# Loads of attention heads with the outermost dimension 64 or 128 in place of 2

## The chip, the cores and the metric

The kernel runs on one core of a Trainium2 chip. The metric is device time of one execution, in microseconds (us). Three runs of the kernel before took 3115.7, 3124.22 and 3126.91 us; their median is 3124.22. A core has five engines with queues of their own: PE (TensorE, matrix products; PEld is its weight load), DVE (VectorE), ACT (ScalarE), POOL (GpSimd) and SP (SyncE, which here only issues transfers). Transfers between the chip's memory and on-chip memory are issued from SP or from POOL and are carried out by 16 DMA engines, which both share.

## The reference

Two decoder layers over 1024 positions of width 1024, in float32. Each layer is a token mixer, a cross-attention into 256 memory rows, and a SwiGLU FFN, with an RMS norm before each and a residual add after. The mixers are:

```python
# layer 0: 8 heads with a sliding window of 128, and 8 MLA heads (dense causal)
s = (jnp.einsum('bqhd,bkhd->bhqk', q_nope[:, q0:q1], k_nope[:, :q1])
     + jnp.einsum('bqhd,bkd->bhqk', q_rope[:, q0:q1], k_rope[:, :q1])).astype(jnp.float32) * scale
p = jax.nn.softmax(jnp.where(causal, s, -jnp.inf), axis=-1).astype(v.dtype)
# layer 1: 16 heads, each a mixture of three dilated windows
DIL_PATTERNS = ((128, 1), (512, 4), (2048, 16))
o, lse = banded_attention(deinterleave(q), deinterleave(k), deinterleave(v), window // dil)
```

Heads are 64 wide; the rotary part of an MLA head is 32 wide (two halves of 16), and its keys are shared by all heads.

## The kernel before, in words

**Precision by splitting.** Each float32 operand x is held as a high part (rounded) and a low part (x minus the high part). A product takes the terms high by high, high by low and low by high. A score is a product over the 64 rows of a head, and PE has 128 rows. So the kernel puts the key's high rows on 64 partitions and its low rows on the other 64 (`kf`), and the query's high rows on all 128, each twice (`q[0]`). One matrix product then gives both terms with the high query; a second one with the query's low rows, again twice (`q[1]`), gives the rest. For an MLA head a third product adds the rotary part: `qr` holds 16 + 16 rotary rows, high and low, each half of them twice, against `KR`. A product is a sum over partitions, so the order of the rows is free as long as keys and queries have the same one.

**Through memory.** Projections write keys to `kd` ([pair of heads, 128 rows, high/low, position]), queries to `qd` ([pair, 128 rows, half, high/low and position]), rotary queries to `qrd`, values to `vd` and `vd1`. The attention then loads them head by head, all with `move` (L175), which issues the transfer on POOL's queue.

**Passes.** The sequence is worked in halves of 512 positions (`hf` 0 and 1): layer 0 first half, layer 0 second half, layer 1 first half, layer 1 second half. In each pass two streams are woven on PE by `g_weave`: "s", attention and the rest of the mixer, and "d", dense work (projections of the other half, or the FFN of the half before). In the rows of the profile `s<-...` and `d<-...` say which stream a product is of. The loads that change belong to:

- `g_mla` (layer 0, 8 heads, both halves): per head one key load, one query load, two rotary loads and one value load, into the tiles `ar` and `qr`;
- `g_att1` (layer 1, first half, 16 heads) and `g_dil` (layer 1, second half, 16 heads): per head one key and one query load, into slices of `tab`, besides value loads.

Scores are at L744 (`g_scores`) and, in `g_dil`, at L1466. Keys and queries have two buffers each, so the load of head n + 1 or n + 2 is issued once the scores of the head before are done.

**What sets the order.** The kernel is written as one sequence; a scheduler with a timing model of its own then orders each engine's queue, and after that every queue runs strictly in order. POOL's queue holds three sorts of work: the issue of its transfers, the low parts of weights (`wl<-wr,wh`, L181 in `lo`), and some scaling in the attention. Weights come through SP's queue (L210), ACT makes the high part (L212) and POOL the low part. Transfers from POOL share eight semaphores in turn (DMASW0 to 7), and each waits for the one eight before it.

Of the kernel before, what the change touches and what calls it, by code (L numbers as in the profile page):

```python
# [19 lines left out]
S = 1024  # L20
# [142 lines left out]
class Builder:  # L163
# [552 lines left out]
    def form_k(self, m, src, n):  # L716

        k = m.kf.next()[:, :n]
        self.move(k, src.rearrange("d j t -> j d t"))
        return k  # L720

    def form_q(self, m, src):

        q = m.q.next().rearrange("p (j t) -> p j t", j=2)
        self.move(q, src[None].to_broadcast([2, 64, 1024]))
        return q[:, 0], q[:, 1]

    def form_v(self, m, src, nb):
# [575 lines left out]
    def g_mla(self, hf):  # L1304

        nc, I, s = self.nc, self.I, self.S
        with ExitStack() as es:
            ext = self.pool(es, f"ml{hf}", 1)
            m = self.att_mem(hf, ext, True)
            W = 512 * (hf + 1)  # L1310
            KR = ext.tile([P, W], F32R, name="KR")
            self.move(KR, self.krd[:, 0:W])
            nc.sync.dma_start(m.bias, I["c_mla"][:, S - W:])

            def head(hd):
                def f():
                    kf = self.form_k(m, self.head(self.kd, 8 + hd, slice(0, W)), W)
                    q = self.form_q(m, self.queries(8 + hd, hf))

                    qr = m.qr.next()  # L1320
                    v = self.qrd[hf, hd // 4].rearrange("(x h) j f t -> h x (j f) t", x=2)[hd % 4]
                    for a in range(2):
                        self.move(qr[64 * a:64 * a + 64], v[a][None].to_broadcast([2, 32, 512]))
                    vf = self.form_v(m, self.vd[8 + hd][:, 0:W // P, :], W // P)
                    return [(q[0], kf), (q[1], kf), (qr, KR)], vf
                return f

            yield from self.g_heads(s, m, hf, [(head(hd), 512 + 64 * hd) for hd in range(8)], m.bias, SC96)
# [14 lines left out]
    def load1(self, m, hd, hf):  # L1343

        if hf:
            k, q = m.kq.next()
            self.move(k, self.head(self.kd, hd, slice(0, S)).rearrange("d j t -> j d t"))
            self.move(q, self.queries(hd, 1)[None].to_broadcast([2, 64, 1024]))
            return k, q.rearrange("p (j t) -> p j t", j=2)
        kf = self.form_k(m, self.head(self.kd, hd, slice(0, 512)), 512)  # L1350
        q = self.form_q(m, self.queries(hd, 0))
        return [(x, kf) for x in q], self.values1(m.vf.next()[:, :512].rearrange("p (b d) -> p b d", d=P), hd, 0)
# [410 lines left out]
```

## Time and profile before

| | |
|---|---|
| median of three runs | 3124.22 us |
| the profiled execution | 3122.54 us, span 3120.6 us |
| mean granted TensorE clock | 0.955 |
| PE busy | 2844.0 us (91%) |
| DVE busy | 1809.0 us (58%) |
| POOL busy | 1489.9 us (48%) |
| ACT busy | 1307.6 us (42%) |
| transfers issued by POOL | 169.92 MB, 18.8% of 16 engines' span |
| transfers issued by SP | 245.67 MB, 27.7% of 16 engines' span |

A row of a group gives line, engine, operation, the tiles written and read, the count, busy time and the mean of one. A row of waits gives who waited, for whom, us in total, times, and the longest. A row of DMA issues gives the tiles, the queue, the count, the size of one transfer and the median time from issue to landing. In a table by windows each row is a stretch of time: its length, then busy time and instructions of each engine, the granted clock of PE, the mean busy share of the 16 DMA engines, and GB/s.

### The profile page before, as it was taken

What the parts mean: (1) busy time and instruction counts of PE and PEld (TensorE: products, weight loads), DVE (VectorE), ACT (ScalarE), POOL (GpSimd) and SP (SyncE); (2) the same over time, 40 slices, a digit from 0 to 9 for tenths busy, and PEclk for the clock granted to TensorE, in tenths of its full rate; (3) what the DMA queues carried; (4) which work ended last, traced back from release to release, by engine and by line L of the source; (5) the groups of instructions that cost most, each with busy time, mean ns of one, the idle gap of its engine ahead of it and who ended that gap; (6) DMA issues with size and microseconds to landing.
All of it is one profiled execution on the core that took longest, in us unless ns stands there. A gap on an engine that the chain in (4) does not pass through costs nothing. (4 is left out here: it accounts for less than half of the span.)

```text
span 3120.6 us, 37882 instructions
## 1 busy us (share of the span) xinstructions
PE 2844.0 (91%) x13500; PEld 2365.7 (76%) x13500; DVE 1809.0 (58%) x3668; ACT 1307.6 (42%) x2539; POOL 1489.9 (48%) x1038
## 2 busy tenths in 40 slices
PE   6866898889999999998899999988889999999998
PEld 5655777768888788876777787866778887878887
DVE  6764766657676564455566646335668865562324
ACT  4644534444443333453444333345455533432222
POOL 3564635554354444644455444444465654444442
PEclk9978999999999999998999999989999999999999
DMA  6666744554453324544555333454555553333331
GB/s 176 173 186 154 224 133 139 144 133 116 119 153 121 109 88 128 165 160 117 131 120 171 115 108 102 144 163 148 129 141 154 137 165 105 109 119 101 95 97 65
DMA packets 467135, 418.00 MB, mean 134 GB/s; under 512 B 114884, under 2 KB 377284, under 8 KB 466948
## 3 DMA queue, kind: packets, MB, share of 16 engines
q1 hardware_dynamic: 333124, 245.67, 27.7%
q0 software_dynamic: 133824, 169.92, 18.8%
q8 instruction: 107, 1.75, 0.2%
q14 instruction: 80, 0.66, 0.1%
HBM read 347.09 MB, written 68.03 MB: 133 GB/s over the span
## 5 line engine op out<-in xcount | busy, mean ns | idle before, releaser
L181 POOL TENSOR_TENSOR wl<-wr,wh 128x1024 fp32r<-128x1024 f32 (+1 forms) x430 | 1036.3, 2417 | 987.6 <-ACT wh L212 924.6
L212 ACT ACTIVATE wh<-wr 128x1024 fp32r<-128x1024 f32 (+1 forms) x418 | 440.4, 1056 | 843.7 <-PE d L236 229.0
L236 PE MATMUL d<-hfh,wh 128*128 128x512 f32 x1408 | 564.1, 401 | 1.8 <-DVE ra L361 1.8
L236 PE MATMUL d<-hfl,wh 128*128 128x512 f32 x1408 | 558.9, 397 | 0.0
L236 PE MATMUL d<-wh,a 128*128 128x512 f32 x1440 | 532.9, 401 | 28.1 <-ACT a L693 13.4
L236 PE MATMUL d<-hfh,wl 128*128 128x512 f32 x1408 | 558.0, 397 | 0.0
L660 DVE TENSOR_TENSOR x<-d,x 128x512 f32<-128x512 f32 x344 | 233.9, 685 | 300.9 <-PE d L236 299.6
L236 PEld LDWEIGHTS d<-wh,a 128*128 128x128 f32 x1440 | 274.4, 191 | 90.2 <-ACT a L693 14.6
L236 PEld LDWEIGHTS d<-hfh,wl 128*128 128x128 f32 x1408 | 269.2, 191 | 54.7
L236 PEld LDWEIGHTS d<-hfh,wh 128*128 128x128 f32 x1408 | 269.2, 191 | 51.1 <-DVE x L660 2.0
L236 PEld LDWEIGHTS d<-hfl,wh 128*128 128x128 f32 x1408 | 269.5, 191 | 49.8 <-issue 0.2
L236 PE MATMUL d<-wl,a 128*128 128x512 f32 x720 | 283.9, 396 | 0.0
L660 DVE TENSOR_TENSOR x<-s,x 128x512 f32<-128x512 f32 x192 | 130.6, 688 | 116.9 <-PE s L236 115.3
L181 DVE TENSOR_TENSOR a<-t,a 128x512 fp32r<-128x512 f32 x104 | 160.5, 1544 | 53.2 <-ACT a L693 51.2
L236 PEld LDWEIGHTS d<-wl,a 128*128 128x128 f32 x720 | 137.7, 191 | 24.8
L757 ACT ACTIVATE af<-af,nm 128x512 f32<-128x512 f32 (+3 forms) x160 | 94.1, 589 | 139.3 <-DVE nm L753 138.8
L687 DVE SCALAR_TENSOR_TENSOR t<-t,d 128x512 f32<-128x512 f32 x88 | 60.2, 685 | 110.2 <-ACT t L686 109.8
L236 PE MATMUL s<-hmh,wl 128*128 128x512 f32 x256 | 103.8, 406 | 20.1 <-POOL wl L181 20.0
L181 DVE TENSOR_TENSOR pl<-s,ph 128x512 fp32r<-128x512 f32 (+1 forms) x158 | 97.4, 629 | 32.8 <-ACT ph L184 32.2
L184 ACT ACTIVATE ph<-s 128x512 fp32r<-128x512 f32 (+1 forms) x158 | 84.2, 550 | 75.5 <-PE s L780 71.7
L753 DVE CUSTOM_DVE_ANT_0 af<-s,bias 128x512 f32<-128x512 f32 (+3 forms) x128 | 67.3, 534 | 79.8 <-PE s L744 50.2
L236 PE MATMUL s<-hmh,wh 128*128 128x512 f32 x256 | 102.5, 400 | 4.9 <-ACT wh L212 4.9
(360 smaller groups left out, 5727.4 us busy)
## 6 DMA issues: line engine op xcount, KB each, us to landing
wr<-in_l_w_gate SPq DMA_DIRECT2D x88, 512.0 KB
wr<-in_l_w_up SPq DMA_DIRECT2D x88, 512.0 KB
wr<-in_l_w_down SPq DMA_DIRECT2D x88, 512.0 KB
wr<-in_l_w_qkv SPq DMA_DIRECT2D x48, 512.0 KB
wr<-in_l_w_out SPq DMA_DIRECT2D x32, 512.0 KB
tab<-qd POOLq DMA_DIRECT2D x32, 512.0 KB, 17.0
ar<-qd POOLq DMA_DIRECT2D x24, 512.0 KB, 17.9
wr<-in_l_w_in SPq DMA_DIRECT2D x22, 512.0 KB
```

Of the source, the lines that this page charges most:

```text
L181: e.tensor_sub(out, x, h.bitcast(F32))
L184: self.nc.scalar.activation(h, ps, AF.Copy)
L212: self.nc.scalar.activation(h, raw, AF.Copy)
L236: self.nc.tensor.matmul(ps, a, b, start=(3 * i + j == 0), stop=(3 * i + j == n - 1))
L660: self.nc.vector.tensor_add(xs, ps, xs)
L687: nc.vector.scalar_tensor_tensor(t, t, 1.0, pg, op0=ALU.add, op1=ALU.mult)
L753: nc.vector.tensor_tensor_reduce(p[:, c:c + n], t, bias[:, b0 + c:b0 + c + n], -scale, lim, ALU.add, ALU.min, accum_out=nm)
L757: nc.scalar.activation(p[:, c:c + n], p[:, c:c + n], AF.Exp, bias=nm, scale=-1.0, accum_out=l[:, i:i + 1])
```

## The change

All loads of keys, queries and rotary queries of a head in `g_mla`, `g_att1` and `g_dil` are issued with another order of rows.

- **Keys.** Before, the source ran over high/low (2), then the head's rows (64). Now it runs over 128 rows, high and low of one row next to each other. Partition 2d holds row d's high part and partition 2d + 1 its low part.
- **Queries.** Before, the source was repeated by an outermost dimension of 2 with a step of zero. Now the repeat stands inside: 64 rows, each read twice.
- **Rotary parts.** Before, two loads per head, each of 32 rows repeated twice by an outermost 2 into 64 partitions. Now four loads of 32 rows into 32 partitions each. The place of the rows is as before.

Bytes, descriptors per row and products are the same; per MLA head there are two more transfers (32 in all).

```diff
     def form_k(self, m, src, n):
         k = m.kf.next()[:, :n]
-        self.move(k, src.rearrange("d j t -> j d t"))
+        self.move(k, src.rearrange("d j t -> (d j) t"))
         return k
 
+    @staticmethod
+    def twice(src):
+
+        return src[:, None].to_broadcast([64, 2, 1024])
+
     def form_q(self, m, src):
         q = m.q.next().rearrange("p (j t) -> p j t", j=2)
-        self.move(q, src[None].to_broadcast([2, 64, 1024]))
+        self.move(q, self.twice(src))
         return q[:, 0], q[:, 1]
...
                     v = self.qrd[hf, hd // 4].rearrange("(x h) j f t -> h x (j f) t", x=2)[hd % 4]
-                    for a in range(2):
-                        self.move(qr[64 * a:64 * a + 64], v[a][None].to_broadcast([2, 32, 512]))
+                    for a in range(4):
+                        self.move(qr[32 * a:32 * a + 32], v[a // 2])
...
         if hf:
             k, q = m.kq.next()
-            self.move(k, self.head(self.kd, hd, slice(0, S)).rearrange("d j t -> j d t"))
-            self.move(q, self.queries(hd, 1)[None].to_broadcast([2, 64, 1024]))
+            self.move(k, self.head(self.kd, hd, slice(0, S)).rearrange("d j t -> (d j) t"))
+            self.move(q, self.twice(self.queries(hd, 1)))
```

The scheduler orders the queues anew. Line numbers from L724 on are five higher in the changed kernel.

On POOL in layer 0, first half, from the second head's loads (`qr_1726`) on, before:

```order
L177 DMA qr_1726<-qrd 64x1x512 x2
L177 DMA ar<-vd 128x512
L181 TENSOR_TENSOR wl<-wr,wh 128x1024
L177 DMA mkv_109<-a_1989 128x256 x2
L181 TENSOR_TENSOR wl<-wr,wh 128x1024
L177 DMA ar<-kd 128x1x512
L177 DMA ar<-qd 128x1x1024
L177 DMA qr_1725<-qrd 64x1x512 x2
L177 DMA ar<-vd 128x512
L815 DMA OTd<-af 64x512
L181 TENSOR_TENSOR wl<-wr,wh 128x1024
```

and now:

```order
L177 DMA qr_1726<-qrd 32x512 x4
L177 DMA ar<-vd 128x512
L181 TENSOR_TENSOR wl<-wr,wh 128x1024 x2
L177 DMA mkv_109<-a_1995 128x256 x2
L177 DMA ar<-kd 128x512
L177 DMA ar<-qd 128x1x1024
L177 DMA qr_1725<-qrd 32x512 x4
L177 DMA ar<-vd 128x512
L177 DMA ar<-kd 128x512
L177 DMA ar<-qd 128x1x1024
L177 DMA qr_1726<-qrd 32x512
L820 DMA OTd<-af 64x512
```

The loads of the third and fourth head now stand together, where a weight's low part stood between them before.

On PE at the same place, where the dense stream turns to the second half's activations (`hBh`, `hBl`), the rows between a tile's first two terms and its third. Before there are 30 rows, of which the first and last are:

```order
L236 MATMUL d<-hBh,wh 128x512
L236 MATMUL d<-hBl,wh 128x512
L744 MATMUL s<-ar 128x384 x2
L744 MATMUL s<-KR,qr_1726 128x384
L628 MATMUL d<-wl,mem 128x512
...
L791 MATMUL s<-ph_1727,ar 128x256
L792 MATMUL s<-ph_1727,ar 128x256
L236 MATMUL d<-hBh,wl 128x512
```

and now there are 50, all of them of stream "s":

```order
L236 MATMUL d<-hBh,wh 128x512
L236 MATMUL d<-hBl,wh 128x512
L796 MATMUL s<-ph_1728,ar 128x256
L797 MATMUL s<-ph_1728,ar 128x128
L785 MATMUL s<-ident,af 128x128 x4
...
L799 MATMUL s<-pl_1730,ar 128x256
L785 MATMUL s<-ident,af 128x128 x4
L236 MATMUL d<-hBh,wl 128x512
```

So for the length of about two heads no dense product stands between the attention's.

In layer 1 POOL's queue keeps its order. Around the load of the second head's queries in the first half it reads, before:

```order
L177 DMA tab<-qd 128x1x1024
L177 DMA qd<-hl 128x1024
L181 TENSOR_TENSOR wl<-wr,wh 128x1024 x3
L177 DMA tab<-kd 128x1x512
L177 DMA tab<-qd 128x1x1024
```

and now:

```order
L177 DMA tab<-qd 128x1x1024
L177 DMA qd<-hl 128x1024
L181 TENSOR_TENSOR wl<-wr,wh 128x1024 x3
L177 DMA tab<-kd 128x512
L177 DMA tab<-qd 128x1x1024
```

Nothing moved there; a store of the last queries (`qd<-hl`) still stands right behind a load.

## The prediction

> **What bounds the kernel now.** I read the page first, then PE's waits.
>
> ```profile
> span 3120.6 us, 37882 instructions
> PE 2844.0 (91%) x13500; PEld 2365.7 (76%) x13500; DVE 1809.0 (58%) x3668; ACT 1307.6 (42%) x2539; POOL 1489.9 (48%) x1038
> ```
>
> PE sets the time, since no other engine is near it; a change that removes no product can win only where PE stands still or runs slowly. It stands still for 3120.6 - 2844.0 = 277 us. Waits of PE over the whole span (who, for whom: us in total, times, longest):
>
> ```profile
> PE s L744 <- DMA ar<-qd: 21.2, 4, 13.4
> PE s L1466 <- DVE de L1468: 15.1, 3, 8.5
> PE d L236 <- ACT wh L212: 14.6, 1, 14.6
> PE d L236 <- ACT a L693: 13.4, 3, 7.7
> PE s L1466 <- DMA tab<-qd: 13.3, 4, 6.7
> PE s L744 <- DMA tab<-qd: 13.3, 3, 6.7
> PE s L744 <- DMA ar<-qrd: 9.7, 1, 9.7
> PE s L744 <- DVE nm L753: 6.9, 1, 6.9
> ```
>
> The rows with DMA are scores that wait for a head's loads: 21.2 + 13.3 + 13.3 + 9.7 = 57.5 us. The others I follow below. Next, how long these loads take (DMA issues; the last column is the median from issue to landing):
>
> ```profile
> tab<-qd POOLq DMA_DIRECT2D x32, 512.0 KB, 17.0
> ar<-qd POOLq DMA_DIRECT2D x24, 512.0 KB, 17.9
> wr<-OTd POOLq DMA_DIRECT2D x16, 512.0 KB, 4.5
> qd<-hl POOLq DMA_DIRECT2D x16, 512.0 KB, 2.9
> tab<-kd POOLq DMA_DIRECT2D x16, 512.0 KB, 16.3
> qr<-qrd POOLq DMA_DIRECT2D x16, 128.0 KB, 16.7
> ```
>
> At equal size from the same queue, those that change take 16 to 18 us, others 3 to 5. DMA queues between 250 and 257 us, when almost only such a load was under way, say why:
>
> ```profile
> q0 software_dynamic: 165, 0.35, 13.7%
> q1 hardware_dynamic: 171, 0.09, 4.2%
> ...
> 1305.00:1306.00 1.00, 1.00 (x6) 0.81 (x5) 0.00 (x0) 0.99 (x2) 1.00 (x1) 1.00 0.98 385
> ```
>
> (The last row is a window, with a store of keys under way; its last two numbers are the DMA engines' share and GB/s. A store has 128 rows outermost, and fills all 16 engines.) POOL's queue q0 used 13.7% of 16 engines, about 2.2 of them, as many as the source's outermost dimension has steps. SP's queue q1, with a weight to bring at the same time, moved 0.09 MB in 7 us: its shares on those two engines take turns with the load's rows, and a weight is there only when its last share is.
>
> So three more of PE's waits belong to the loads. The chain of waits (start, us, what) has the store in front of the dilated pass, and a weight there beside one outside it:
>
> ```profile
> 2158.26 11.80 DMA qd<-hl
> ...
> 2292.67 13.64 DMA wr<-in_l_w_up
> ...
> 2562.17 3.62 DMA wr<-in_l_w_out
> ```
>
> POOL's timeline around the first, and SP's in the pass before:
>
> ```profile
> 2154.14 0.83 POOL L177 DMA_DIRECT2D tab<-qd  x1 [2.31 <-DVE t L508]
> ...
> 2158.26 0.56 POOL L177 DMA_DIRECT2D qd<-hl  x1 [0.86 <-DVE hl L181]
> 2170.71 3.09 POOL L177 DMA_DIRECT2D v<-vd  x5 [11.89 <-DMA qd<-hl]
> ...
> 1414.84 0.82 POOL L177 DMA_DIRECT2D tab<-qd  x1
> 1417.54 0.56 POOL L177 DMA_DIRECT2D qd<-hl  x1 [1.88 <-DVE hl L181]
> ...
> 1431.90 0.34 SPq L1420 DMA_DIRECT2D bias<-in_c_dil  x1
> ```
>
> A store issued behind a query load took 11.80 us in place of 2.9, and what reuses its room waited: at 2171 us the 8.5 of "DVE de L1468", at 1435 us, through the mask's load, the 6.9 of "DVE nm L753". The weight that took 13.64 us ends in the 7.7 of "ACT a L693"; the 14.6 of "ACT wh L212" is the weight that crawled at 250 us. Together 8.5 + 6.9 + 7.7 + 14.6 = 37.7 us, and with the direct waits 95.2.
>
> Last, the clock. Four stretches, each right behind a stall but the first, which is one (length; busy; granted clock sixth):
>
> ```profile
> 212.21:225.65 13.44, 0.00 (x1) 0.03 (x1) 0.00 (x0) 1.06 (x1) 0.66 (x1) 0.60 0.63 132
> 225.65:242.30 16.65, 11.80 (x42) 9.74 (x43) 11.06 (x20) 4.71 (x12) 10.50 (x11) 0.50 0.79 159
> 259.25:262.90 3.65, 3.65 (x10) 3.12 (x11) 2.98 (x6) 1.49 (x6) 2.36 (x1) 0.51 0.05 14
> 282.70:286.70 4.00, 4.00 (x17) 3.81 (x18) 0.78 (x2) 1.19 (x2) 3.59 (x3) 0.50 0.44 105
> 670.00:1110.00 440.00, 421.15 (x2123) 354.32 (x2122) 269.75 (x528) 181.71 (x356) 185.97 (x120) 0.98 0.44 122
> ```
>
> After stalls of 13.4, 14.6 and 6.7 us PE ran at half clock for 16.65, 3.65 and 4.0 us, which costs half of that, 12.1 us for 34.7 of stall: 0.35 us for each us.
>
> **The change, part by part.** *Keys and queries.* 48 heads load both. With 64 or 128 steps outermost I expect all 16 engines and the landing of the spread rows: 512 KB in 2.9 to 4.5 us, so a pair in about 6 where it took 18. The source of a query with a repeat of 2 inside is a form that no row of before has; its bounds are 4.5 us and the 17.9 of now, and I take 4.5, as its outermost dimension is that of the stores. The Trainium skill, page "DMA: Bandwidth & Descriptors", section "Why a DMA increments its semaphore by 16 and not by 1", says a transfer takes the largest number of engines up to 16 that divides the outermost size on both sides. By it the old loads get 2, as the trace shows, and the new 16.
>
> The issues cost POOL less, if anything (least, median, most in ns):
>
> ```profile
> L177 POOL DMA_DIRECT2D tab<-vd x64: 548/552/785, 1267.8 to 1679.3; - x64
> L177 POOL DMA_DIRECT2D tab<-qd x32: 782/810/978, 1321.5 to 2447.2; - x32
> L177 POOL DMA_DIRECT2D qr<-qrd x16: 653/664/886, 205.8 to 326.8; - x16
> L177 POOL DMA_DIRECT2D qd<-hl x16: 559/572/698, 1309.9 to 2158.3; - x16
> ```
>
> At the store's 572 ns 48 queries give back 48 x 0.24 = 11 us of POOL, at 810 nothing.
>
> *Rotary loads.* 32 more issues at 552 to 664 ns are 18 to 21 us of POOL in layer 0. They lie in time in which POOL is idle (it is busy for 186 of the 440 us from 670 on) and PE has the dense stream; without that cover they would cost these 21 us. Each transfer waits for the one eight before it, and a head now has seven and not five. Landing in 6 us at most, against eight issues of 0.6, that does not bind; at today's 17 it would, and does now:
>
> ```profile
> POOL qr L177 <- DMA ar<-qd: 21.0, 3, 9.3
> ```
>
> Against the split speaks the same page, section "Rules for kernel authors": small transfers are mostly overhead, and halves of the partitions are better moved in one. By its fixed 2.0 us, paid one after the other, two more loads cost 4 us a head, an estimate, seen by PE only at the first head of each half: 8 us less gain.
>
> *Order.* Layer 1 keeps POOL's order, so there the stalls can go with nothing else moved. In layer 0 the first half is woven anew, with 50 rows of attention in one piece, where PE has nothing to fill the softmax's latency.
>
> *The sum*, in gaps plus 0.35 of them for the clock:
> - layer 0, first half: 21.2 + 14.6 = 35.8, with clock 48. I take half, 24, for the new order.
> - layer 0, second half: 9.7, with clock 13. I take 10; the first load is issued just before its use and still needs some 6 us.
> - layer 1, first half: 13.3 + 6.9 = 20.2, with clock 27.
> - layer 1, second half: 13.3 + 8.5 + 7.7 = 29.5, with clock 40.
>
> Of the last two I take three quarters, 20 + 30, between the ends: all of it, and half of the direct waits alone, without clock (29 us over all passes). The nearer row is the one from 670 to 1110 us: the same sort of loads, issued a head early, and beyond the first load's 9.7 PE stands still for 9 of 440 us. What is late next is the softmax's chain on DVE, which is why it is not all. Sum: 24 + 10 + 20 + 30 = 84 us; 3122.5 - 84 = 3038.5 for the profiled execution, which ran 1.7 us below the median of the runs. I predict 3040.
>
> **The rivals.**
> *Another engine takes over.* In the dilated pass DVE is the next:
>
> ```profile
> 2146.00:2483.00 337.00, 296.60 (x1516) 255.12 (x1515) 240.23 (x635) 175.93 (x463) 179.83 (x157) 0.93 0.55 142
> ```
>
> It is busy for 240 of 337 us, and PE already waits for it there (15.1 above). If a DVE wait steps into each gap's place, half of the direct waits return and no clock: 3122.5 - 29 = 3094. Against it: 71% leaves a quarter free. 0.16.
>
> *The queries stay on few engines*, because the repeat inside counts. Then keys and rotary parts are quick, but the score still waits for the queries; issued 0.8 us behind the keys, they now end the waits. About a quarter of the ceiling of 128 returns, from lighter traffic on the two engines: 3122.5 - 32 = 3091; with queues no better, 3110. 0.05.
>
> *Slower.* Layer 0's new order decides: weights' low parts stand behind two heads of loads (14 issues x 0.65 = 9 us), and the dense stream, cut off for two heads, comes late. If each of the eight heads of the first half got a gap like the 14.6 with its clock, 20 us, that is 160 in place of the 48 there now: 112 lost, against 60 gained elsewhere, about 3175. It decides from the point where the first half grows by more than layer 1 gives back, some 50 us. Against it: the dense products only move within the pass, and the loads that delayed POOL get short. 0.04.
>
> *No change*: the scores wait as long for something not seen. 0.05.
>
> **How the numbers follow.** The forecast holds 0.70: its own range is 2994 (the whole ceiling of 95.2 x 1.35 = 128) to 3080. With the case of 3094 the range is 2992 to 3095. A measurement here tells 0.5%, 16 us: faster means below 3108.6. Forecast, most of the takeover and the queries' case lie there: 0.91. Within: 0.05. Slower: 0.04.
>
> **What would show it.** The issue rows of `tab<-qd`, `ar<-qd` and `tab<-kd` at 3 to 7 us, and q0's share up in short bursts; PE's waits on DMA down from 57.5 to below 15; the store before the dilated pass near 3 us; weights there at 4; the clock's mean from 0.955 to 0.97 or more. Landing rows that stay near 17 for queries show the second rival; quick landings with PE waiting for DVE rows instead show the first. The prediction is wrong if loads land fast and the time stays above 3095.

## The result and the profile after

The changed kernel takes **2977.94 us** (median of 4 runs, 2975.36 to 2979.06) against 3121.96 us for the kernel before in the same runs: a ratio of **0.9539**, 95% interval 0.9519 to 0.9558. The forecast was 3040, range 2992 to 3095. The sign was right; 144 us were gained, not 84, and also more than the 128 that the prediction held to be all there was.

From the page of the changed kernel, the span and the engines:

```profile
span 2976.7 us, 37929 instructions
PE 2819.6 (95%) x13500; PEld 2350.7 (79%) x13500; DVE 1790.7 (60%) x3668; ACT 1309.3 (44%) x2539; POOL 1478.8 (50%) x1070
```

PE's idle time fell from 276.6 to 157.1 us. The other 24.4 us are PE's busy time, 2844.0 to 2819.6 for the same 13500 products: the granted clock (mean 0.955 before, 0.973 now). PE's waits over the whole span (who, for whom: us in total, times, longest), the largest, the dilated pass's, and all on heads' loads:

```profile
PE s L399 <- DVE xn L416: 39.1, 14, 9.0
...
PE s L1471 <- DVE de L1473: 7.2, 2, 4.3
...
PE s L749 <- DMA ar<-qrd: 1.7, 1, 1.7
...
PE s L1254 <- DMA ar<-qd: 0.7, 1, 0.7
...
PE s L749 <- DMA qr<-qrd: 0.7, 1, 0.7
```

(Lines after L724 moved by five: L744 is L749 now, L1466 is L1471.) The 57.5 us of direct waits on loads that the prediction counted (59.4 with two more rows of 1.6 and 0.3) became 3.1. The DMA issues, last column the median from issue to landing:

```profile
tab<-qd POOLq DMA_DIRECT2D x32, 512.0 KB, 5.6
ar<-qd POOLq DMA_DIRECT2D x24, 512.0 KB, 7.4
...
tab<-kd POOLq DMA_DIRECT2D x16, 512.0 KB, 5.0
...
qr<-qrd POOLq DMA_DIRECT2D x32, 64.0 KB, 6.3
```

Keys and queries of 512 KB land in 5 to 7 us where they took 16 to 19, the queries with their repeat inside too. (8 of the 24 loads in the row `ar<-qd` are of the sliding-window heads and did not change.)

**Where the time went.** Stretches between the same instructions in both kernels (length; busy time and instructions of PE, PEld, DVE, ACT, POOL; granted clock; DMA share; GB/s): layer 0 first half, layer 0 second half, layer 1 first half, layer 1 second half (attention stages). Before:

```profile
198.10:674.30 476.20, 395.32 (x1899) 328.60 (x1898) 294.81 (x628) 210.05 (x438) 241.72 (x201) 0.89 0.56 157
674.30:1307.10 632.80, 610.59 (x2978) 510.49 (x2977) 366.00 (x682) 251.32 (x459) 282.84 (x174) 0.98 0.45 126
1307.10:1682.30 375.20, 329.50 (x1540) 270.58 (x1539) 215.45 (x431) 165.22 (x315) 183.19 (x162) 0.94 0.49 132
2044.60:2516.90 472.30, 415.79 (x2036) 351.31 (x2035) 311.14 (x739) 244.09 (x572) 248.39 (x210) 0.93 0.53 143
```

and after:

```profile
201.50:659.50 458.00, 403.63 (x1909) 330.29 (x1908) 286.89 (x631) 213.12 (x440) 246.01 (x218) 0.91 0.54 164
659.50:1284.10 624.60, 610.22 (x2969) 509.60 (x2968) 360.34 (x680) 250.46 (x456) 283.65 (x190) 0.99 0.41 127
1284.10:1591.70 307.60, 306.30 (x1534) 258.42 (x1533) 210.13 (x431) 165.06 (x315) 175.26 (x163) 1.00 0.52 162
1954.80:2373.70 418.90, 402.99 (x2036) 344.34 (x2035) 312.42 (x739) 243.55 (x572) 240.21 (x210) 0.99 0.52 161
```

Against the prediction's terms:

| stage | predicted | measured | of it idle time | of it busy time |
|---|---|---|---|---|
| layer 0, first half | 24 | 18.2 | 26.5 | -8.3 |
| layer 0, second half | 10 | 8.2 | 7.8 | 0.4 |
| layer 1, first half | 20 | 67.6 | 44.4 | 23.2 |
| layer 1, second half | 30 | 53.4 | 40.6 | 12.8 |
| elsewhere | 0 | -3.5 | | |
| sum | 84 | 143.9 | | |

Layer 1 gave 121 of the 144. Its first half shows why the count was short. PE's waits there, before, the seven largest:

```profile
PE s L744 <- DMA tab<-qd: 13.3, 3, 6.7
PE s L744 <- DVE nm L753: 6.9, 1, 6.9
PE s L236 <- POOL wl L181: 6.6, 4, 3.8
PE d L236 <- ACT a L693: 5.6, 2, 3.2
PE s L791 <- ACT ph L184: 3.8, 1, 3.8
PE s L793 <- DVE pl L181: 3.5, 2, 1.8
PE s L236 <- ACT wh L212: 2.4, 3, 1.7
```

and all that is left of them:

```profile
PE d L236 <- DVE a L181: 0.7, 1, 0.7
PE d L236 <- DVE t L687: 0.6, 1, 0.6
```

The prediction had counted the first two rows, 20.2 us. The other five name POOL, ACT and DVE, come to 21.9 us, and went as well, though nothing was changed on these engines.

What these engines themselves waited for in layer 1, up to the end of the dilated pass (1307.1 to 2516.9 us before, 1284.1 to 2373.7 after), went too. ACT waited 93.8 us for weights to land, the largest row "ACT wh L212 <- DMA wr<-in_l_w_up: 64.9, 12, 9.4", and now 15.2. POOL stood 34.5 us before loads until a store of queries had landed ("POOL tab L177 <- DMA qd<-hl: 22.6, 2, 14.0" and 11.9 of `v`), and now 9.1.

### The profile page after: what moved, and what is told of

It is laid out like the page before. It is cut to its first block, busy times and chain, and to the rows that moved or that the text cites. A ratio compares the mean times of both kernels' runs of the same rounds, so it can differ in the third digit from the quotient of the medians.

```text
span 2976.7 us, 37929 instructions
## 1 busy us (share of the span) xinstructions
PE 2819.6 (95%) x13500; PEld 2350.7 (79%) x13500; DVE 1790.7 (60%) x3668; ACT 1309.3 (44%) x2539; POOL 1478.8 (50%) x1070
## 5 line engine op out<-in xcount | busy, mean ns | idle before, releaser
L212 ACT ACTIVATE wh<-wr 128x1024 fp32r<-128x1024 f32 (+1 forms) x418 | 440.1, 1056 | 738.9 <-PE d L236 248.2
L181 DVE TENSOR_TENSOR pl<-s,ph 128x512 fp32r<-128x512 f32 (+1 forms) x158 | 97.7, 631 | 46.7 <-ACT ph L184 46.0
L399 PE MATMUL s<-ident,xn 128*128 128x128 f32 x384 | 62.8, 310 | 41.9 <-DVE xn L416 39.1
L236 PE MATMUL s<-hml,wh 128*128 128x512 f32 x256 | 100.3, 392 | 0.0
```

Of the source, the lines that this page charges most:

```text
L181: e.tensor_sub(out, x, h.bitcast(F32))
L212: self.nc.scalar.activation(h, raw, AF.Copy)
L236: self.nc.tensor.matmul(ps, a, b, start=(3 * i + j == 0), stop=(3 * i + j == n - 1))
L399: self.nc.tensor.transpose(v[:, k, :], xn[:, (k0 + k) * P:(k0 + k + 1) * P], self.ident)
```

## The experiments

Two questions were left. Did those waits on other engines go because of the loads, although no engine waited for a load there? And why did layer 0 give so little?

### One layer alone

Layer 1 as changed, layer 0's loads as before (`layer1_only`). Every product on PE stands in the order of the kernel before.

```diff
 # in g_mla
-                    kf = self.form_k(m, self.head(self.kd, 8 + hd, slice(0, W)), W)
-                    q = self.form_q(m, self.queries(8 + hd, hf))
+                    kf = m.kf.next()[:, :W]
+                    self.move(kf, self.head(self.kd, 8 + hd, slice(0, W)).rearrange("d j t -> j d t"))
+                    q = m.q.next().rearrange("p (j t) -> p j t", j=2)
+                    self.move(q, self.queries(8 + hd, hf)[None].to_broadcast([2, 64, 1024]))
+                    q = q[:, 0], q[:, 1]
...
-                    for a in range(4):
-                        self.move(qr[32 * a:32 * a + 32], v[a // 2])
+                    for a in range(2):
+                        self.move(qr[64 * a:64 * a + 64], v[a][None].to_broadcast([2, 32, 512]))
```

> Layer 1's loads as in the change, layer 0's as before. Theory: layer 1's two passes give 67 and 53 us by the marks of the two traces, whatever layer 0 does: 3122 - 120 = 3002 us, within 6. Rival (part of layer 1's gain is carried over from layer 0, for instance by the place at which the streams meet): 3020 or more.

Measured: 3004.46 us, ratio 0.9618 (0.9596 to 0.9639), within the theory's 6 us. With nothing moved in PE's order, layer 1's loads alone are worth 119 us. So layer 1's gain owes nothing to a new order.

### Two-engine copies that nobody waits for

To the changed kernel, one copy of the head's queries into a spare tensor per head and half of layer 1, 512 KB each, 32 in all. In `extra2` the outermost dimension is 2, as the old loads had it; in the control `extra64` it is 64; in `extra2_act` the two-engine copies are issued from ScalarE, so that they stand in a queue of their own.

```diff
+            self.move(self.spare[hf, hd], self.queries(hd, hf)[None].to_broadcast([2, 64, 1024]))   # extra2
+            self.move(self.spare[hf, hd], self.twice(self.queries(hd, hf)))                         # extra64
+            self.nc.scalar.dma_start(...)     # extra2_act: as extra2, from ScalarE's queue
```

> The changed kernel plus, for each head and half of layer 1, a copy of the head's queries (twice, 512 KB) into a tensor that nobody reads, with an outermost dimension of 2: the old loads' confinement to two DMA engines with no engine waiting for it. 32 copies, 16.8 MB. Theory (a two-engine transfer takes turns with the weights on the same engines and stretches them, and so costs the 24 us of waits in layer 1's first half that the profile put on ScalarE, VectorE and GpSimd and that went with the loads): 3000 to 3040, weights landing in over 8 us instead of 4, and the loss is in layer 1's two attention stages. Rival (only a wait on the load itself costs anything): within 8 us of the control with the same copies over 16 engines.

> The control to the run with the extra two-engine copies: the same 32 copies of the same bytes at the same places, with an outermost dimension of 64. The order of TensorE's work is the same in both. Theory: the bytes alone cost little, 2975 to 2995; what the other run takes above this one is the price of the two engines alone, with no direct wait in it.

> The run with the 32 extra two-engine copies in layer 1 (3079 us; its control over 16 engines 2984), with the copies issued by ScalarE into its own DMA queue instead of GpSimd's: no store and no load of a head stands behind a copy in a queue any more, and what is left is that two DMA engines are shared with the weights and everything else. The scheduler's order of layer 1 differs a little, and ScalarE has 32 issues more. Theory 1 (the sharing of the engines does most of the harm): 3040 to 3085, and weights still wait. Theory 2 (standing in the same queue does it: stores that take 16 us instead of 6 and the loads behind them): 2980 to 3005, with the stores of keys and queries back at 3 to 6 us. In between the loss divides accordingly.

Measured: `extra64` 2983.60 us (0.9561, 0.9547 to 0.9576), `extra2` 3078.73 (0.9867, 0.9852 to 0.9881), `extra2_act` 3163.19 (1.013, 1.0092 to 1.0168). The bytes cost some 6 us (the intervals overlap, and PE's order in layer 1 is not quite the changed kernel's); the same bytes on two engines cost 95 us more, with every engine's queue in the same order; from a queue of their own some 180 us more than the control. The 95 us lie far beyond the 3000 to 3040 of `extra2`'s theory: the mechanism was expected, its size was not. Two thirds of the change's gain are given back by copies whose data nobody uses; a single wait on a copy, 6.1 us of a store on POOL, is in the trace.

PE's waits from 1280 to 2500 us in `extra2`, the rows that grew most and the one on a load:

```profile
PE s L236 <- ACT wh L212: 23.9, 9, 4.6
PE s L1473 <- DVE de L1475: 21.0, 3, 13.2
PE s L236 <- POOL wl L181: 16.0, 10, 2.3
PE s L796 <- ACT ph L184: 9.3, 1, 9.3
...
PE s L1473 <- DMA tab<-qd: 4.4, 1, 4.4
```

and in the control:

```profile
PE s L1473 <- DVE de L1475: 13.0, 4, 4.3
...
PE s L236 <- POOL wl L181: 6.8, 7, 2.3
...
PE s L236 <- ACT wh L212: 0.2, 1, 0.2
```

Only 4.4 of the 95 us stand in a row that names a load. The rest stands in rows of ACT, DVE and POOL, the sorts of rows that the prediction had left out, and in the clock. Two paths show. One is the queue. The DMA issues of `extra2`:

```profile
spare<-qd POOLq DMA_DIRECT2D x32, 512.0 KB, 14.8
...
kd<-hl POOLq DMA_DIRECT2D x16, 512.0 KB, 15.8
qd<-hl POOLq DMA_DIRECT2D x16, 512.0 KB, 11.1
```

The stores of keys and queries took 6.4 and 3.9 us in the control. They stand behind a copy. POOL's queue, being in order, then stands still as well, where a copy is issued only when a store of queries has landed. POOL's waits from 1280 to 2500 us in `extra2` hold the row

```profile
POOL spare L177 <- DMA qd<-hl: 89.9, 12, 10.7
```

and the control's is 19.0 us. So much of it belongs to the experiment: in the kernel before, waits of this sort came to the 34.5 us above. The other path is the two engines. In `extra2_act` no store stands behind a copy and the two kinds of store land in 7.1 and 6.9 us, but ACT's and SP's waits from 1270 to 2600 us are

```profile
ACT wh L212 <- DMA wr<-in_l_w_qkv: 119.0, 14, 18.4
...
SPq L210 <- DMA wr<-in_l_w_qkv: 114.9, 12, 16.5
```

and PE waits 99.1 us for the high parts of weights:

```profile
PE s L236 <- ACT wh L212: 99.1, 14, 16.5
```

The chain of waits there (start, us, what) shows single weights that take 27 and 33 us:

```profile
1298.29 32.60 DMA wr<-in_l_w_qkv
...
1334.54 26.69 DMA wr<-in_l_w_qkv
```

From 1316 to 1320 us, with nothing but copies and the rest of a weight under way, the queues (packets, MB, share of 16 engines) were

```profile
q10 hardware_dynamic: 46, 0.19, 11.4%
q1 hardware_dynamic: 45, 0.02, 1.8%
```

q10 is ScalarE's queue: 11.4% of 16 engines is 1.8 engines, and the weights' queue q1 moved 0.02 MB in 4 us, about one packet of its own, of 512 B, for each of the copies', of 4 KB. So theory 1 of that run held, beyond the loss that it gave (3040 to 3085): sharing two engines does harm without a queue in common. The 180 us are not all its doing, though. PE's order in layer 1 differs from the control's. And ACT, which makes the weights' high parts, was itself held by the issue of its copies: 10 of the 32 took 1.1 to 12.0 us in place of 0.58, together 43 us more, for a reason that no row gives. Why the copies do more harm from ScalarE's queue than from GpSimd's, where they also have to wait behind stores and loads, no run tells. Nor is it shown how PE's loss in layer 1 of the kernel before divided between the two paths.

The idle time that `extra2` adds to the control in layer 1's two stages, and the busy time that comes with it (`extra2` first, then the control):

```profile
1277.50:1635.60 358.10, 320.30 (x1532) 265.19 (x1532) 209.33 (x429) 164.21 (x315) 188.10 (x178) 0.95 0.53 162
1999.90:2472.10 472.20, 419.46 (x2033) 353.71 (x2032) 316.56 (x739) 243.90 (x572) 253.24 (x226) 0.93 0.52 161
```

```profile
1281.00:1591.30 310.30, 306.75 (x1532) 259.19 (x1531) 215.71 (x430) 163.86 (x315) 184.97 (x178) 0.99 0.61 187
1954.80:2380.60 425.80, 404.43 (x2036) 343.53 (x2035) 314.84 (x739) 243.67 (x572) 249.75 (x225) 0.98 0.58 178
```

Idle 90.5 against 24.9 us, busy 739.8 against 711.2: 28.6 us of clock for 65.6 of gaps, 0.44 us for each. In layer 1 of the change itself it is 36.0 for 85.0, 0.42. The prediction's 0.35 was near; it counted the 16.65 us behind the first stall whole, of which PE was busy for 11.80, and by busy time it would have been 0.28.

### Queries alone

The kernel before with only the queries changed, to two loads of 64 rows (`queries_only`).

```diff
-        self.move(q, src[None].to_broadcast([2, 64, 1024]))
+        for j in range(2):
+            self.move(q[64 * j:64 * j + 64], src.rearrange("p (j t) -> p j t", j=2))
```

> Queries alone in two loads of 64 rows; keys and rotary parts as before, outermost 2. Theory: the queries' 17 us go to 5, the keys' stay at 10 to 16 us and end the scores' wait, a little earlier than the queries did, and the two engines' traffic halves: 50 to 80 us of the 144 return, 3040 to 3070 us. Rival (only the last lander counts, and that is now the key): 3100 or more. Other rival (the queries were the whole of it): below 3000.

Measured: 3080.13 us, ratio 0.9864 (0.9845 to 0.9884), between the forecasts. With more query loads the scheduler also came to another order of PE's work in both layers, and what that cost or gave is not told apart. Issues of this run:

```profile
tab<-qd POOLq DMA_DIRECT2D x64, 256.0 KB, 12.7
...
tab<-kd POOLq DMA_DIRECT2D x16, 512.0 KB, 17.6
```

A query load on all 16 engines, behind a key load on two in the same queue, still lands in 12.7 us, where 5.4 is seen behind quick ones (next run). That it is the key ahead of it that keeps it is inferred from the two numbers.

### Keys and queries in halves

The changed kernel with each key and query load split in two of 64 rows, in the old row order (`halves`): all 16 engines by another way, and 96 issues more. The scheduler's order is again another, in both layers.

```diff
-        self.move(k, src.rearrange("d j t -> (d j) t"))
+        for j in range(2):
+            self.move(k[64 * j:64 * j + 64], src[:, j])
```

> All loads of keys and queries in two loads of 64 rows each, outermost 64, so that the rows keep the order of before (high rows, then low rows); rotary parts as in the change. Theory: the interleaving is only a means, 16 engines are reached this way too, and 96 more issues of some 0.55 us lie in POOL's idle time: the change's 2978 us, within 10. Rival (small transfers into halves of the partitions cost as much as they bring, as each pays its own fixed time): 2 us more per head, 3040 or more with the eight transfers in flight used up.

Measured: 2991.91 us, 0.9583 (0.9563 to 0.9603), 14 above the changed kernel, a little outside the 10. The spread over engines is what counts in the main, and not how it is come by: 256 KB of queries land in 5.4 us, no sooner than 512 KB in one load. In the profiled run the loss lies in and around the dilated pass, where PE waits 13.0 us for "DVE de" against 7.2. The rule of the Trainium skill that the prediction weighed (page "DMA: Bandwidth & Descriptors", section "Rules for kernel authors", against halves of the partitions) points the same way, but this run cannot bear it out: the 14 us may be the 96 issues (0.15 us each, if they are all theirs) or the new order.

### Layer 0: the rotary loads or the order

The changed kernel's PE order in layer 0 is not the one of the kernel before. In the traces `rot_old` and `rot_64` have, product by product, the order of the kernel before, and `rot_two` and `rot_new_only` the changed kernel's. That allows a table. `rot_old` is the changed kernel with the old rotary loads; `rot_new_only` the kernel before with the four new ones; `rot_64` has two loads of 64 rows, and `rot_two` four loads with an outermost dimension of 2 (both read other rows of the same group).

```diff
 # rot_old
-                    for a in range(4):
-                        self.move(qr[32 * a:32 * a + 32], v[a // 2])
+                    for a in range(2):
+                        self.move(qr[64 * a:64 * a + 64], v[a][None].to_broadcast([2, 32, 512]))
 # rot_64
+                    v = self.qrd[hf, hd // 4].rearrange("(h x) j f t -> h (x j f) t", x=2)[hd % 4]
+                    for a in range(2):
+                        self.move(qr[64 * a:64 * a + 64], v)
 # rot_two
+                    v = self.qrd[hf, hd // 4].rearrange("(x h) j f t -> h j x f t", x=2)[hd % 4]
```

> The change with its rotary loads put back to two per MLA head, outermost 2. Theory (what counts is on how many of the 16 DMA engines a transfer lies): layer 0 alone loses, and little, since a rotary load is 128 KB on its two engines and not 512; 5 to 15 us over the change, so 2983 to 2993 us. Rival (layer 0's new order of the queues is what held its gain down, and the two extra loads caused that order): at or below the change's 2978.

> The kernel before with one part of the change alone: a head's rotary queries in four loads of 32 rows instead of two with a repeat in front; keys and queries as before. With the four loads the program's order of TensorE's work is the one of the changed kernel, with two it is the one of the kernel before, so this run, the kernel before (3123), the changed kernel (2978) and the changed kernel with two rotary loads (2959) make a square. Theory: the four loads cost layer 0 some 20 us through that order, whatever the keys and queries do: 3135 to 3150. Rival 1: under the old loads the order does nothing and the shorter rotary loads pay a little: 3105 to 3120. Rival 2: order and rotary loads are nothing by themselves, 3118 to 3128; then the 19 us come only together with the faster keys and queries.

> The changed kernel with each head's rotary part in two loads of 64 rows of their own, without repeat, from the same stored group but from the wrong rows of it: the output is not the reference's, the bytes and the arithmetic are the same. Two loads per head give TensorE the order of the kernel before in every place, so this is that order with rotary loads over 16 engines. The run with two old rotary loads took 2959 us, the changed kernel 2978. Theory (the order of layer 0 is what the changed kernel pays 19 us for): 2948 to 2963, a few us under the run with old rotary loads, whose rotary loads TensorE still waited for once (3.9 us). Rival (the way the rotary rows are loaded makes the 19 us): 2968 to 2985.

> The changed kernel with its four rotary loads per head taken from two rows of blocks 256 KB apart instead of one run of 32 rows, so that each has an outermost dimension of 2 (other rows of the same group, the output is not the reference's): the order of TensorE's work is the changed kernel's in every place, the rotary loads are back on two engines. Theory (the order costs 19 us, the rotary loads' engines little): 2976 to 2992. Rival (the rotary loads make the difference, and slow ones are the better ones because they leave the other engines free): under 2968. A third way: slow rotary loads in the new order stand in the way of the keys behind them on the queue, 2995 to 3020.

| us (ratio to before, interval) | order of the kernel before | order of the changed kernel |
|---|---|---|
| old keys and queries, old or new rotary loads | before: 3118 to 3123 | `rot_new_only` 3132.15 (1.0042, 1.0027 to 1.0058) |
| new keys and queries, rotary on two engines | `rot_old` 2958.89 (0.9471, 0.9447 to 0.9495) | `rot_two` 2979.74 (0.9542, 0.9517 to 0.9567) |
| new keys and queries, rotary on 16 | `rot_64` 2948.84 (0.9439, 0.9415 to 0.9464) | changed: 2977.94 (0.9539, 0.9519 to 0.9558) |

`rot_old` was expected by its theory at 2983 or above and came out 19 us under the changed kernel, as its rival had it: the theory that the rotary split helps fell. `rot_64` and `rot_two` then part the two things that the split does, and both came out as their theories said. `rot_new_only`, under the slow loads, came out 14 us above the kernel before, between its theory (3135 or more) and its rival (3128 or less). The new order costs 21 us (middle row) to 29 (last row); the rotary loads' spread wins 10 in the old order (the runs lie apart, the intervals overlap a little) and nothing measurable in the new. The landings: of 128 KB, 9.1 to 9.3 us on two engines (`rot_old`) and 6.8 to 7.6 over 16 (`rot_64`); of 64 KB, 6.2 to 7.1 (`rot_two`) and 6.3 to 6.4 (changed). The order changed only together with the number of rotary loads, two or four a head, so a cost of the two further loads themselves is not parted from it. The cost stands in layer 0 alone. From the load of the rotary keys to the first load of x, and from there to the load of the FFN's norm, in the changed kernel:

```profile
201.50:329.00 127.50, 106.27 (x479) 85.48 (x478) 66.63 (x172) 58.41 (x126) 70.47 (x91) 0.84 0.64 194
329.00:506.20 177.20, 152.40 (x673) 121.26 (x672) 127.31 (x230) 76.79 (x143) 85.27 (x64) 0.92 0.53 169
```

and in `rot_64`:

```profile
195.40:313.60 118.20, 98.40 (x509) 82.65 (x508) 76.78 (x186) 62.10 (x134) 66.22 (x77) 0.91 0.71 210
313.60:481.60 168.00, 141.10 (x641) 114.47 (x639) 120.83 (x214) 72.22 (x133) 82.74 (x62) 0.94 0.54 177
```

Both are 9 us longer in the changed kernel, by clock (0.84 against 0.91) rather than by idle time: over these two stretches 46.0 us idle against 46.7, and 19 us more of busy time for 1152 products against 1150. That speaks for the order and against waits on the further loads. The rest of the 29 us lies in layer 0's second half. The changed kernel scatters its idle time: at 219, 239, 243 and 254 us stand gaps of 2 to 4 us, where `rot_64` has one of 3.6 and one of 9.2. That the spread of gaps sets the clock is an inference; no run changed the gaps alone. The Trainium skill (page "TensorE: Matmul & The Clock Gate", section "Part 1: The HAM clock gate") fits it: it says that the clock follows PE's activity in free-running windows of some 3.4 us. If so, several short gaps can cost as many half-clock windows as one long one.

### A faster version

Two versions keep two rotary loads a head, 64 rows each without a repeat, by storing the rotary queries twice. `rot_dup` needs two more stores per group. `rot_all` needs one store in place of two, with another row order in memory, and loads the rotary keys in the matching order.

```diff
 # rot_all
-            for j in range(2):
-                self.move(self.qrd[hf, g, :, j], t[:, j])
+            u = t.rearrange("p j t -> p (j t)")
+            self.move(self.qrd[hf, g], u[:, None].to_broadcast([128, 2, 1024]))
...
-            self.move(KR, self.krd[:, 0:W])
+            for x in range(2):
+                self.move(KR[64 * x:64 * x + 64], self.krd[64 * x:64 * x + 64, 0:W].rearrange("(r f) t -> f r t", r=4))
...
-                    v = self.qrd[hf, hd // 4].rearrange("(x h) j f t -> h x (j f) t", x=2)[hd % 4]
-                    for a in range(4):
-                        self.move(qr[32 * a:32 * a + 32], v[a // 2])
+                    v = self.qrd[hf, hd // 4].rearrange("(x h f) r (j t) -> h x (f r j) t", x=2, h=4, j=2)[hd % 4]
+                    for a in range(2):
+                        self.move(qr[64 * a:64 * a + 64], v[a])
```

> The changed kernel with the rotary queries stored twice in memory, so that each head's rotary part is again two loads, each of 64 rows of their own with no repeat: as few loads as before, none on two DMA engines; 64 KB more is written with each group of rotary queries, in two more stores. The scheduler gives layer 0 an order that is neither that of the kernel before nor that of the changed kernel. Theory (layer 0's order decides there, and it is luck which one the scheduler comes to): layer 0 lands anywhere between the two, 2955 to 2985, and the rest of the program stays within 5 us of the changed kernel's. Rival (what costs the changed kernel 19 us are its four loads themselves, 2.5 us each to issue and land together, not the order): 2940 to 2960, and no wait on a rotary load over 1 us.

> A version that computes the reference: the changed kernel with the rotary queries stored twice, by one store per group instead of two, and laid out so that a head's rotary part is two loads of 64 rows without a repeat; the rotary keys are loaded in two loads with their rows in the matching order. No load of a head has an outermost dimension below 16. The scheduler gives layer 0 another order again, alike up to the first rotary store only. Theory (the order of layer 0 decides, by chance): 2945 to 2985, layer 1 within 5 us of the changed kernel's. Rival (fewer loads and stores are what counts): under 2955.

Measured: `rot_dup` 2969.11 us (0.9506, 0.9486 to 0.9526), `rot_all` **2950.01** (0.9444, 0.942 to 0.9468). `rot_all` computes what the reference does and is 28 us under the changed kernel. Each has an order of layer 0 of its own, and their layer 1 agrees with the changed kernel's within 5 us. `rot_dup` lies in the range of its theory (the order) and outside that of its rival (the four loads themselves, 2940 to 2960), though it also has more stores. `rot_all` has fewer stores and lies in its rival's range as well as in its theory's, and the two are not told apart for it.

## Why the prediction was too small

**PE sets the time, and the loads hold it up through two DMA engines: right.** Of the direct waits 3.1 us are left, and loads land as forecast (5.0 to 5.6 us for the rows of `tab`; `ar<-qd` at 7.4 is just above the 7 named).

**"Its shares on those two engines take turns with the load's rows, and a weight is there only when its last share is" (SP's queue): right, and counted far too low.** This is the step that failed. The prediction followed this mechanism to four waits (37.7 us), and then took 128 us for "the whole ceiling". In layer 1 the waits counted were 20.2 + 29.5 = 49.7 us of idle time; 85.0 went. The 35.3 between them stood in rows of POOL, ACT and DVE that it did not count. One was not small. In the list of PE's waits over the whole span, from which the prediction shows eight rows, the third is missing there:

```profile
PE s L236 <- POOL wl L181: 21.2, 11, 9.7
```

Of it 20.0 us stood in layer 1's two stages (6.6 and 13.4), and 3.9 are left.

**"Of the last two I take three quarters, 20 + 30": wrong.** It kept a quarter for the softmax's chain on DVE as the next limit. In layer 1's first half nothing was next: 1.3 us of idle time are left in 307.6. In the second half "DVE de" and "DVE dx" keep 7.2 and 3.4 us. The row from 670 to 1110 us, on which the choice leaned, was in layer 0. The 71 us that layer 1's terms (50) fell short of the measured 121 are thus: 17 for the quarter, 35 for the waits not counted, and 19 of clock on these and by the higher factor (36.0 in all, against 0.35 x 49.7 = 17.4).

**"I take half, 24, for the new order": right in sense, a little high.** The half was a choice, and that it came near is in part luck. Layer 0's first half gave 18. In the order of the kernel before (`rot_64`) the same stretch, from 195.4 to 634.6 us, is 37 shorter than before, against the ceiling of 48; the second half gave 8 of the 10. The rival "slower" was right that the new order costs something, 21 to 29 us, but not in its price of 112, nor in its mechanism of a long gap at each head: against `rot_64` PE's idle time in the two stretches above is the same, and its products run slower.

**The rotary issues: hidden, right.** The rotary issues take 0.57 us each (median), and POOL's busy time fell all the same. Of the 21.0 us that POOL waited before rotary loads no row is left; 5.4 stand before other loads of heads ("POOL ar L177 <- DMA ar<-qd"). "That does not bind" was a little too strong, since eight issues of 0.6 us are 4.8 and the landing was put at 6. What the split costs, it seems to cost through the order, which the prediction saw changing, but not as the split's doing: it was priced as a thing of layer 0 as a whole.

**The queries' inner repeat: 5.6 us, taken at 4.5, bounds 4.5 to 17.9.** The rule of the Trainium skill on the outermost size (page "DMA: Bandwidth & Descriptors", section "Why a DMA increments its semaphore by 16 and not by 1") agrees: at 512 KB, 64 outermost with a repeat inside lands in 5.6 us and 128 rows in 5.0, and what has 2 outermost took 14.8 to 18.5. A query issue costs 612 ns in the dilated pass, from 810: 0.20 us less where 0.24 was the most.

**The other rivals.** DVE did not take over: its row in the dilated pass fell from 15.1 to 7.2 us. The queries did not stay on few engines. The store ahead of the dilated pass is in the chain with 4.53 us, from 11.80, forecast near 3; the clock's mean is 0.973, forecast 0.97 or more.

## What to carry to other kernels

A transfer confined to two DMA engines can cost more through the transfers that share its engines or its queue than through those that wait for it: in layer 1 here 26.6 us of the 85.0 named a load. Look for loads whose landing time is several times that of others of their size, and allow for the waits on weights, and on whatever is stored or loaded behind them, as theirs too, whichever engine the row names. Before adding transfers to a program that a scheduler orders, see what they do to the order; a version with the same bytes in fewer transfers, that keeps the order, may be worth more than their speed.

## What the runs showed of the hardware

*Tiny packets.* The pages' rows of packets, before and after:

```profile
DMA packets 467135, 418.00 MB, mean 134 GB/s; under 512 B 114884, under 2 KB 377284, under 8 KB 466948
```

```profile
DMA packets 385216, 417.61 MB, mean 140 GB/s; under 512 B 32964, under 2 KB 295364, under 8 KB 385028
```

The same rows moved with 81,920 fewer packets below 512 B, 640 for each of the 128 loads changed. It goes with two engines on GpSimd's queue: `extra2` has 62,148 such packets and its control 33,476, 896 for each copy, while `extra2_act`, with the same copies from ScalarE's queue, has 33,028 and moved them in 4,160 packets of about 4 KB, 130 each. What the tiny packets are for no row says. The harm does not need them: `extra2_act` has no more of them than the control and is the slowest.

*Landing time hardly depended on size* here once a load was spread: 512 KB 5.0 us, 256 KB 4.4 (`tab<-kd`), 64 KB 4.0 (`tab<-vd`) and 6.3 (`qr<-qrd`). Some loads that the change didn't touch halved too (`tab<-vd` from 8.0, `wh<-vd` of 512 KB from 10.2 to 4.4), others did not (`x<-xd`, 6.1 and now 6.4).
